# Layer 0's output product on two float16 parts for 28 of its 32 steps, with the weights' squares summed ahead

## The chip, the core and the metric

The kernel runs on one NeuronCore of a Trainium2 chip. The metric is the device time of one execution in microseconds; the median of three timed runs before the change is 1795.62 us (1794.34 to 1796.36). A core has a matrix engine (TensorE, PE in the profile; its weight loads are listed as PEld), a vector engine (VectorE, DVE), an activation engine (ScalarE, ACT), a general engine (GpSimd, POOL), a queue engine that mostly issues transfers (SyncE, SP), and 16 DMA engines shared by all queues. Each engine takes its instructions in the order of its own queue and waits on semaphores.

## The reference, cut to what matters

Two layers of a prefix model over 256 tokens and 256 context tokens, width 2048, branch width 4096. Layer 0 is a Fourier mixer, layer 1 an attention mixer. The change lies in the end of layer 0: the gate `silu(z)` and the output product `y @ w_out[0]`.

```
def _fourier_branch(h, w_in, w_mix):
    u, z = jnp.split(h @ w_in, 2, axis=-1)
    ...
    f = jnp.einsum('bngc,gcd->bngd', f, w_mix).reshape(b, n, D_BRANCH)
    return f * jax.nn.silu(z)

def reference(...):
    for i in range(DEPTH):
        shift, scale, gate = jnp.split((jax.nn.silu(c) @ ada_w[i] + ada_b[i])[:, None, :], 3, axis=-1)
        ...
        x = x + gate * (y @ w_out[i])
        if need_ctx:
            xc = xc + gate_c * (yc @ w_out[i])
    return _rmsnorm(x, final_g)
```

All is float32. The kernel keeps that accuracy on the matrix engine by writing each operand as a high part and a low part and summing three products (high x high, high x low, low x high).

## The kernel before, in words

**Products in parts.** `mm3` (lines 132 to 135) issues the three matmuls, 128x128 stationary by 128x512 moving (256 tokens of x beside 256 of the context). Two kinds of parts are in use. The float32r kind (`split`, `half_split`, lines 65 to 73): ACT casts to the high part (L66), DVE subtracts for the low part (L67); a half weight tile of 128x1024 takes two slots of the pool `wsp`, which has six. The float16 kind (`split16`, lines 122 to 127): ACT scales and casts (L125), DVE multiplies and subtracts (L126); both parts of a half tile share one slot. Float16 has few exponent bits, so it needs a power-of-two scale first: `squares` sums the squares of a weight tile on ACT (L81), `as_b` casts the sums to bfloat16 (L86), `all_sum` adds them over the partitions with small matmuls against ones (L93) into a PSUM tile of its own, and `weight_scale` makes the scale and its inverse with three tiny DVE operations (L117 to L119).

**The gate product (lines 802 to 874).** For each of 32 blocks of 128 branch columns, z = W_z^T h, on float16 parts. The first four blocks share weight tiles; then block b has its own 1 MB tile in the pool `raw` (three slots), loaded and squared two blocks ahead (`z_load`). A step is 16 k times three matmuls. At k = 6 of step b the scale of block b + 1 is made. `z_out` (L817 on) takes Silu of z on ACT (L820), multiplies the mixer's y by it on DVE (L821), and then draws a unit of the adaptive modulation. The results `ys` stay in the pool `yp`, 32 tiles of 128x512 float32.

**The modulation units (`ada_jobs`, lines 757 to 785).** 64 units, drawn by `next(ada)`. A unit loads 1 MB of the modulation weights (two tiles `zr` and `wa` in the gate stage, one `raw` tile later) and reduces it on DVE against rows of silu(c): four reductions of 128x1024 (L780), only two where the piece is the last (i = 3). The rows `cb` are loaded by POOL.

**The output product (lines 877 to 941).** 32 steps: two sweeps of 16, each over all 4096 rows of half of w_out's columns. Step i loads one `raw` tile of 1 MB, splits it to float32r parts (four `wsp` slots), and multiplies it with the parts of two tiles of y into eight PSUM tiles, all eight banks. `y_split0` makes these parts (L66 and L67 at 128x512) in slots of the pool `act` (33 slots, shared with the gate's h parts and temporaries), one step ahead, and again in the second sweep. In the last step of a sweep `evac0` adds each bank times the gate `gt0` to x on DVE and squares the result on ACT. From the twelfth step of a sweep on, POOL loads tiles of x. `ada_rate` says how many modulation units a step draws.

**Order.** Instructions get their places on an engine's queue by a list scheduler when the program is built; `tc.issue_after(ins)` forces what stands in the block behind `ins` on the same engine.

Of the kernel before, what the change touches and what calls it, by code (L numbers as in the profile page):

```python
# [17 lines left out]
P = 128  # L18
# [14 lines left out]
def tile_dit(ctx: ExitStack, tc: tile.TileContext, a: dict, out: bass.AP):  # L33
# [21 lines left out]
    def act(dt=F32):  # L55
        return actp.tile([P, 512], dt, tag="act", name="act")
# [8 lines left out]
    def split(h, l, src, eng=V):  # L65
        last_cast[0] = S.copy(h, src).ins  # L66
        last_sub[0] = eng.tensor_tensor(l, src, h.bitcast(F32), op=ALU.subtract).ins  # L67
# [47 lines left out]
    def weight_scale(b, ea):  # L115
        x, up, dn = tiny(I32), tiny(), tiny()
        V.tensor_scalar(x, all_sum(b).bitcast(I32), 24, 23, op0=ALU.logical_shift_right, op1=ALU.logical_shift_left)  # L117
        V.tensor_scalar(up.bitcast(I32), x, -1.0, 204.0 * 2**23, op0=ALU.mult, op1=ALU.add)  # L118
        V.tensor_scalar(dn.bitcast(I32), x, ea, 2.0**23, op0=ALU.add, op1=ALU.max)  # L119
        return up, dn  # L120

    def split16(t, i, up):
        w = wsp.tile([P, 2, 1024], F16, tag="ws", name="wf")
# [5 lines left out]
    def ws_split(t):  # L129
        return [half_split(t, i) for i in range(2)]  # L130
# [626 lines left out]
    def ada_jobs():  # L757
        for pieces in ((0,), (1, 2, 3)):
            for kh in range(2):
                cb = adap.tile([P, 2, 1024], F32, tag="cb", name="cb")  # L760
                with tc.issue_after(hs_end[2]):
                    nc.gpsimd.dma_start(cb, a["crow"][:, kh].broadcast_to([P, 2, 1024]))
                with tc.issue_after(hs_end[1]):
                    S.activation(cb, cb, AF.Silu)
                for i in pieces:
                    for fg in range(8):
                        for f in range(2):
                            q = slice(f * 1024, f * 1024 + 1024)
                            if f == 0 and not out0[0]:
                                wf = adat.tile([P, 1024], F32, tag="zr", name="zr", bufs=2)  # L770
                                nc.sync.dma_start(wf, a["adw"][i, kh, fg][:, q])
                            elif not out0[0]:
                                wf = wsp.tile([P, 1024], F32, tag="ws", name="wa")
                                nc.sync.dma_start(wf, a["adw"][i, kh, fg][:, q])
                            else:
                                if f == 0:
                                    w = raw(a["adw"][i, kh, fg])
                                wf = w[:, q]
                            for s in range(2 if i < 3 else 1):
                                V.tensor_tensor_reduce(junk if s == 0 and i < 3 else wf, wf, cb[:, s], 1.0, 0.0, ALU.mult, ALU.add, acc[:, i, kh, fg * 2 + f, s : s + 1])  # L780
                        if kh == 1 and fg == 7:
                            ada_done(i)
                        yield
        while True:
            yield
# [5 lines left out]
    adat = lay0.enter_context(tc.tile_pool(name="adat", bufs=1))  # L791
    junk = adat.tile([P, 1024], F32, name="junk")
    acc = adat.tile([P, 4, 2, KT, 2], F32, name="acc")
    with tc.tile_pool(name="yp", reuse_waits="tile", bufs=32) as ypool:
        ys = []
        for b in range(NB):
# [5 lines left out]
        def make_hs(k):  # L802
# [10 lines left out]
                hs_end[0] = V.scalar_tensor_tensor(l[:, q], t, sh0[:, k, s : s + 1], h[:, q], op0=ALU.add, op1=ALU.subtract).ins  # L813
            hs.append((h, l))

        if True:
            def z_out(b, o, dn):  # L817
                y = ys[b]
                z = act()
                S.activation(z, o, AF.Silu, scale=dn)  # L820
                V.tensor_tensor(y, y, z, op=ALU.mult)  # L821
                if b >= 4:
                    with tc.issue_after(hs_end[0]) if b < 8 else nullcontext():
                        for _ in range(0 if b in (12, 20) else 1):
                            next(ada)

            zt, sc, sb = {}, {}, {4 + i: as_b(nrm[:, 38 + 2 * i : 40 + 2 * i]) for i in range(2)}

            def z_load(b):
                if b < NB:  # L830
                    zt[b] = raw(a["wz"][b - 4])
                    if b > 5:
                        sb[b] = squares(zt[b], b)

            o4 = [psum() for _ in range(4)]
            for kg in range(4):
                wr = raw(a["wz0"][kg])
                w = []
                for i in range(2):
                    make_hs(kg * 4 + i * 2)  # L840
                    with tc.issue_after(hs_end[0]) if kg else nullcontext(), tc.issue_after(hs_end[1]) if kg else nullcontext():
                        w.append(split16(wr, i, up4))
                    make_hs(kg * 4 + i * 2 + 1)
                if kg == 3:
                    z_load(4)
                    sc[4] = weight_scale(sb[4], ea)
                for j in range(4):
                    k = kg * 4 + j
                    wh, wl = w[j // 2]
                    for b in range(4):  # L850
                        q = slice((j % 2) * 512 + b * P, (j % 2) * 512 + (b + 1) * P)
                        mm3(o4[b], wh[:, q], wl[:, q], hs[k][0], hs[k][1], k == 0, k == KT - 1)
            for b in range(4):
                with tc.issue_after(last_dma[0]):
                    nc.sync.dma_start(ys[b], fd[b])
            for b in range(4):
                z_out(b, o4[b], dn4)
            z_load(5)
            for b in range(4, NB):
                t, (up_, dn_) = zt.pop(b), sc.pop(b)  # L860
                w = [split16(t, i, up_) for i in range(2)]
                z_load(b + 2)
                with tc.issue_after(last_dma[0]):
                    nc.sync.dma_start(ys[b], fd[b])
                o = psum()
                for k in range(KT):
                    if k == 6 and b + 1 < NB:
                        with tc.issue_after(r):
                            sc[b + 1] = weight_scale(sb[b + 1], ea)
                    wh, wl = w[k // 8]  # L870
                    q = slice((k % 8) * P, (k % 8 + 1) * P)
                    r = mm3(o, wh[:, q], wl[:, q], hs[k][0], hs[k][1], k == 0, k == KT - 1)
                z_out(b, o, dn_)
            out0[0] = True


        x1, sqs = [], []
        yy = {}

        def y_split0(i):  # L880
            for j in range(2):
                h, l = act(F32R), act(F32R)
                split(h, l, ys[i % 16 * 2 + j])
                yy[i, j] = (h, l)

        def evac0(k, o):
            t = xin.pop(0)
# [18 lines left out]
        xin, sq_end, st_end, sums = [], [None], [None], []  # L906
        identr = act(F32R)[:, 0:P]
        S.copy(identr, ident)
        ada_rate = {2: 2, 4: 2, 6: 2, 8: 2, 10: 2, 14: 0, 15: 0, 16: 0, 18: 2, 20: 2, 22: 2, 25: 2, 26: 2, 27: 2, 28: 2, 29: 0, 30: 0, 31: 0}
        y_split0(0)  # L910
        for i in range(32):
            sw, kg = i // 16, i % 16
            if kg == 0:
                o = [psum() for _ in range(8)]
            w = ws_split(raw(a["wo0"][sw, kg]))
            if i < 31:
                y_split0(i + 1)
            else:
                wr = raw(a["wkv"][0])
                w0 = half_split(wr, 0)  # L920
            if kg >= 12:
                for k in range(sw * 8 + (kg - 12) * 2, sw * 8 + (kg - 12) * 2 + 2):
                    t = act()
                    nc.gpsimd.dma_start(t, a["xT"][:, k, :])
                    xin.append(t)
            with tc.issue_after(last_sub[0]) if i < 2 or 11 < i < 19 else nullcontext():
                for _ in range(ada_rate.get(i, 1)):
                    next(ada)
            edge = kg in (0, 15)
            for j, b in [(j, b) for b in range(8) for j in range(2)] if edge else [(j, b) for j in range(2) for b in range(8)]:  # L930
                q = slice(b * P, (b + 1) * P)
                last = i == 31 and (j, b) == (1, 7)
                if last:
                    sums.append(psum())
                    with tc.issue_after(e):
                        row_sums(0)
                        row_sums(1)
                with tc.issue_after(st_end[0]) if last else nullcontext():
                    e = mm3(o[b], w[j][0][:, q], w[j][1][:, q], *yy[i, j], kg + j == 0, kg * 2 + j == NB - 1)
                if kg == 15 and j == 1:  # L940
                    evac0(sw * 8 + b, o[b])
# [628 lines left out]
```

## Time and profile before

| | us |
|---|---|
| median of three timed runs | 1795.62 |
| the profiled execution, its own time | 1790.85 |
| its span (first to last instruction) | 1789.1 |
| gate product, from the Silu of the first blocks to that of the last | 372.15 to 661.10 |
| output product, first sweep | 662.55 to 838.50 |
| output product, second sweep | 838.50 to 1012.90 |

The profile is of one execution. A row for an instruction gives its start, its duration, the engine and the line, what it writes and reads, and in brackets how long the engine sat idle before it and what ended that. A row for a group gives the sum of its time, the mean of one in ns, and the idle time before. A matmul's duration includes the time in which the next already runs, so the distance from start to start is its price. A stretch gives the busy time of each engine between two times.

### The profile page before, as it was taken

Reading aid. Unit: us, or ns where it says so; the run is one execution under the profiler, and the core shown is the slowest. Engines: PE = TensorE matmul, PEld = TensorE weight load, DVE = VectorE, ACT = ScalarE, POOL = GpSimd, SP = SyncE. Lnnn points to the kernel's source line nnn. Section 1 sums busy time; section 2 is a strip of 40 time slices with the busy share of each in tenths; the row PEclk is TensorE's granted clock in tenths of the full one; section 3 lists DMA queues with packets and bytes.
Section 4 is the critical chain, followed back from the end, with each engine's and each line's share of the span. In section 5 each row is a group of like instructions: output and inputs, shape, how many; then the busy total and the mean of one; then the engine's idle time right before and its main releaser. Section 6 shows DMA issues by size and latency. Waiting matters only on the chain.

```text
span 1789.1 us, 25928 instructions
## 1 busy us (share of the span) xinstructions
PE 1752.3 (98%) x9514; PEld 1340.9 (75%) x9514; DVE 1399.3 (78%) x2406; ACT 977.5 (55%) x1701; POOL 213.5 (12%) x214
## 2 busy tenths in 40 slices
PE   6999999999999999999999999999999999999997
PEld 4679999544444448888888888788888878887886
DVE  5779888787776779776996563899999999997455
ACT  5545555464555453224222443687788778886343
POOL 0001111100000000000001000322213221234010
PEclk9999999999999999999999999999999999999999
DMA  9998998766666645863678322578888888887543
GB/s 394 417 353 256 274 278 237 300 229 216 232 211 238 227 143 212 321 243 118 227 267 321 119 94 99 173 198 213 219 200 207 212 212 206 213 213 269 192 168 142
DMA packets 210720, 405.16 MB, mean 226 GB/s; under 512 B 152672, under 2 KB 153072, under 8 KB 178848
## 3 DMA queue, kind: packets, MB, share of 16 engines
q1 hardware_dynamic: 186528, 365.49, 63.2%
q0 software_dynamic: 19920, 31.06, 6.8%
q10 hardware_dynamic: 4144, 6.95, 1.1%
q8 instruction: 75, 1.23, 0.3%
q14 instruction: 53, 0.43, 0.1%
HBM read 358.35 MB, written 12.59 MB: 207 GB/s over the span
## 4 chain that ended last, share of the span: by engine, by line
PE 57%; DVE 6%; DMA 4%; issue 2%; ACT 1%; SPq 0%; POOLq 0%; DVEq 0%; POOL 0%; ACTq 0%
PE ps L133 14%; PE ps L135 14%; PE ps L134 14%; PE ps L1234 5%; PE ps L1236 3%; DMA wa<-in_adw 2%; DMA ft<-f 1%; PE ps L1305 1%; PE ps L1270 1%; PE ps L1271 1%; PE ps L1306 1%; DVE junk L780 1%; DVE wl L67 1%; DVE f L1288 1%; DVE ps L1272 1%
## 5 line engine op out<-in xcount | busy, mean ns | idle before, releaser
L67 DVE TENSOR_TENSOR wl<-raw,wh 128x1024 fp32r<-128x1024 f32 x269 | 349.3, 1305 | 171.3 <-ACT wh L66 162.2
L66 ACT CAST wh<-raw 128x1024 fp32r<-128x1024 f32 x269 | 280.5, 1046 | 286.7 <-PE ps L134 198.8
L133 PE MATMUL ps<-act,wh 128*128 128x512 f32 x512 | 198.4, 390 | 1.5 <-ACT act L66 1.5
L134 PE MATMUL ps<-act,wh 128*128 128x512 f32 x512 | 199.2, 389 | 0.0
L134 PE MATMUL ps<-act,wf 128*128 128x512 f16 x512 | 194.0, 379 | 0.0
L135 PE MATMUL ps<-act,wf 128*128 128x512 f16 x512 | 191.0, 379 | 1.4 <-DVE wf L126 1.3
L133 PE MATMUL ps<-act,wf 128*128 128x512 f16 x512 | 189.8, 379 | 1.1 <-ACT act L812 0.3
L1234 PE MATMUL ps<-h,wh 128*128 128x512 f32 x512 | 184.8, 396 | 0.0
L135 PE MATMUL ps<-act,wl 128*128 128x512 f32 x512 | 184.2, 389 | 0.0
L1236 PE MATMUL ps<-h,wl 128*128 128x256 f32 x512 | 138.6, 281 | 0.0
L125 ACT ACTIVATE wf<-raw,tn 128x1024 f16<-128x1024 f32 x64 | 70.1, 1140 | 105.8 <-DVE tn L118 103.1
L134 PE MATMUL ps<-wl,h 128*128 128x512 f32 x320 | 126.7, 396 | 0.0
L135 PE MATMUL ps<-wh,h 128*128 128x512 f32 x320 | 125.3, 395 | 0.0
L133 PE MATMUL ps<-wh,h 128*128 128x512 f32 x320 | 124.0, 402 | 0.0
L133 PEld LDWEIGHTS ps<-act,wh 128*128 128x128 f32 x512 | 96.0, 188 | 22.1 <-ACT act L66 2.0
L1288 DVE SCALAR_TENSOR_TENSOR f<-p,sm,f 128x512 f16<-128x512 f32 x128 | 104.5, 836 | 9.5 <-ACT f L1287 9.2
L134 PEld LDWEIGHTS ps<-act,wh 128*128 128x128 f32 x512 | 96.1, 188 | 20.1
L135 PEld LDWEIGHTS ps<-act,wl 128*128 128x128 f32 x512 | 96.1, 188 | 19.9
L1234 PEld LDWEIGHTS ps<-h,wh 128*128 128x128 f32 x512 | 96.2, 188 | 18.9
L1275 ACT ACTIVATE p<-ps,mx 128x512 f32<-128x512 f32 x128 | 87.9, 689 | 38.3 <-DVE mx L1272 32.2
L1287 ACT ACTIVATE f<-p,sm 128x512 f16<-128x512 f32 x128 | 87.8, 717 | 31.6 <-DMA ft<-f 13.6
L126 DVE SCALAR_TENSOR_TENSOR wf<-raw,tn,wf 128x1024 f16<-128x1024 f32 x64 | 79.6, 1280 | 30.7 <-ACT wf L125 30.7
(372 smaller groups left out, 4160.7 us busy)
## 6 DMA issues: line engine op xcount, KB each, us to landing
raw<-in_wz SPq DMA_DIRECT2D x64, 1024.0 KB, 5.1
raw<-in_adw SPq DMA_DIRECT2D x38, 1024.0 KB, 6.1
raw<-in_awp SPq DMA_DIRECT2D x32, 1024.0 KB, 12.8
raw<-in_wo SPq DMA_DIRECT2D x32, 1024.0 KB, 5.1
raw<-in_wq SPq DMA_DIRECT2D x32, 1024.0 KB, 5.0
raw<-in_wu SPq DMA_DIRECT2D x32, 1016.0 KB, 6.6
raw<-in_wo1b SPq DMA_DIRECT2D x16, 1024.0 KB, 4.9
zr<-in_adw SPq DMA_DIRECT2D x26, 512.0 KB, 4.0
```

The lines of the kernel that those rows point to most:

```text
L66: last_cast[0] = S.copy(h, src).ins
L67: last_sub[0] = eng.tensor_tensor(l, src, h.bitcast(F32), op=ALU.subtract).ins
L125: last_cast[0] = S.activation(w[:, 0], src, AF.Copy, scale=up).ins
L126: last_sub[0] = V.scalar_tensor_tensor(w[:, 1], src, up, w[:, 0], op0=ALU.mult, op1=ALU.subtract).ins
L133: PE.matmul(o, wh, xh, start=start, stop=False)
L134: PE.matmul(o, wh, xl, start=False, stop=False)
L135: return PE.matmul(o, wl, xh, start=False, stop=stop).ins
L1234: PE.matmul(o[0], wh[:, q], hx1[k], start=k == 0, stop=k == KT - 1)
L1236: PE.matmul(o[0][:, 0:N], wl[:, q], hx1[k][:, 0:N], start=False, stop=False)
L1275: S.activation(pt[tb], so[tb], AF.Exp, bias=mx[:, tb : tb + 1], scale=-1.0, accum_out=sm[:, tb : tb + 1])
L1287: S.activation(f[:, 0:512], pt[tb], AF.Copy, scale=sm[:, tb : tb + 1])
L1288: V.scalar_tensor_tensor(f[:, 512:1024], pt[tb], sm[:, tb : tb + 1], f[:, 0:512], op0=ALU.mult, op1=ALU.subtract)
```

## The change

Steps 0 to 13 of each sweep (28 of 32) use float16 parts for the weights and for y; steps 14 and 15 keep float32r. One scale serves all weights of a sweep and one serves all y, so that the products of a sweep can be summed in the same banks. y's parts in steps 14 and 15 are multiplied by both scales, and `gt0` takes the inverse.

To know the scales in time, the weights of w_out are loaded a first time by POOL in half tiles (two pieces of 128x512 each, into `act` slots) and squared with a sum on ACT: 36 half tiles beside the gate product (one after even blocks, two after odd, blocks 4 to 27), 28 in steps 0 to 13 of the first sweep. The squares of y 0 to 27 are summed behind `z_out`. The first sweep's sums are made in gate steps 29 and 30, the second sweep's in step 14.

The float16 parts of y are kept for the second sweep, in place of y itself. The parts of steps 0 and 1 are made in gate step 31. The scale of gate block b + 1 is made at k = 1 in place of k = 6. The last 24 modulation units are put in another order, so that a unit with two reductions comes between those with four, and `ada_rate` is given anew (38 units in the 32 steps, as before).

```
+    def sum_scale(b):
+        s, x, up = tiny(), tiny(I32), tiny()
+        V.tensor_scalar(s, all_sum(b), 2.0**-70, None, op0=ALU.max)
+        V.tensor_scalar(x, s.bitcast(I32), 24, 23, op0=ALU.logical_shift_right, op1=ALU.logical_shift_left)
+        V.tensor_scalar(up.bitcast(I32), x, -1.0, 204.0 * 2**23, op0=ALU.mult, op1=ALU.add)
+        return x, up
...
+                order = [(i, fg) for i in pieces for fg in range(8)]
+                if kh == 1 and len(pieces) == 3:
+                    thirds = [(3, fg) for fg in range(8)]
+                    order = order[:4] + [o for pair in zip(order[4:12], thirds) for o in pair] + order[12:16]
...
+    def scan_sums():
+        while pend:
+            t, j = pend.pop(0)
+            S.activation(t, t, AF.Square, accum_out=scn[:, j : j + 1])
+
+    def scan_loads(n):
+        for j in [next(scans) for _ in range(n)]:
+            for q in range(2):
+                t = act()
+                c = (j % 2 * 2 + q) * 512
+                nc.gpsimd.dma_start(t, a["wo0"][j // 32, j % 32 // 2][:, c : c + 512])
+                pend.append((t, j * 2 + q - 64 * (j >= 36)))
...
+    def half_scale(sw, sums_):
+        x, up = sum_scale(sums_[0])
+        if sw == 0:
+            xy, uy = sum_scale(sums_[1])
+            keep(ysc[:, 0:1].bitcast(I32), xy)
+            keep(ysc[:, 1:2], uy)
+        up_ = keep(ysc[:, 2 + 3 * sw : 3 + 3 * sw], up)
+        both, dn = ysc[:, 3 + 3 * sw : 4 + 3 * sw], ysc[:, 4 + 3 * sw : 5 + 3 * sw]
+        V.tensor_tensor(both, up_, ysc[:, 1:2], op=ALU.mult)
+        V.tensor_scalar(dn.bitcast(I32), x, ysc[:, 0:1].bitcast(I32), -27.0 * 2**23, op0=ALU.add, op1=ALU.add)
+        return up_, both, dn
...
+        def y_split0(i):
+            for j in range(2):
+                k = i % 16 * 2 + j
+                if k < 28:
+                    if i < 16:
+                        t = (ypool if k else actp).tile([P, 1024], F16, tag="y" if k else "act", name="y")
+                        h, l, up = t[:, 0:512], t[:, 512:1024], ysc[:, 1:2]
+                    else:
+                        yy[i, j] = yy[i - 16, j]
+                        continue
+                else:
+                    h, l, up = act(F32R), act(F32R), osc[i // 16][1]
+                last_cast[0] = S.activation(h, ys[k], AF.Copy, scale=up).ins
+                last_sub[0] = V.scalar_tensor_tensor(l, ys[k], up, h if k < 28 else h.bitcast(F32), op0=ALU.mult, op1=ALU.subtract).ins
+                yy[i, j] = (h, l)
...
                 V.tensor_tensor(y, y, z, op=ALU.mult)
+                if b < 28:
+                    ysq[b] = z
+                for i in [i for i in ysq if i < b]:
+                    S.activation(ysq.pop(i), ys[i], AF.Square, accum_out=scn[:, 72 + i : 73 + i])
...
-                    if k == 6 and b + 1 < NB:
+                    if k == 1 and b + 1 < NB:
                         with tc.issue_after(r):
                             sc[b + 1] = weight_scale(sb[b + 1], ea)
+                    if (k, b) == (4, 29):
+                        with tc.issue_after(r):
+                            hsum = half_sum(0)
+                    if (k, b) == (12, 30):
+                        with tc.issue_after(r):
+                            osc.append(half_scale(0, hsum))
+                    if (k, b) == (10, 31):
+                        with tc.issue_after(r):
+                            y_split0(0)
+                            y_split0(1)
...
                 z_out(b, o, dn_)
+                scan_sums()
+                scan_loads(1 + b % 2 if b < 28 else 0)
...
-        ada_rate = {2: 2, 4: 2, 6: 2, 8: 2, 10: 2, 14: 0, 15: 0, 16: 0, 18: 2, 20: 2, 22: 2, 25: 2, 26: 2, 27: 2, 28: 2, 29: 0, 30: 0, 31: 0}
-        y_split0(0)
+        ada_rate = {**{i: 2 for i in (*range(6, 10), *range(17, 25))}, **{i: 0 for i in (14, 15, 16, 29, 30, 31)}}
...
-            w = ws_split(raw(a["wo0"][sw, kg]))
-            if i < 31:
+            wr = raw(a["wo0"][sw, kg])
+            w = [split16(wr, j, osc[sw][0]) for j in range(2)] if kg < 14 else ws_split(wr)
+            if sw == 0:
+                scan_sums()
+                scan_loads({0: 3, 3: 3, 6: 1, 7: 1, 8: 1, 9: 1, 10: 3, 12: 3}.get(i, 2) if i < 14 else 0)
+            if i == 14:
+                osc.append(half_scale(1, half_sum(1)))
+            if kg == 14:
+                q = gt0[:, sw * 8 : sw * 8 + 8].rearrange("p k s -> p (k s)")
+                V.tensor_scalar(q, q, osc[sw][2], None, op0=ALU.mult)
+            if i in range(1, 31):
                 y_split0(i + 1)
```

`half_sum` reduces the columns of the sums on DVE and casts them for `all_sum`; `keep` is a copy of one column; a rate not given is 1.

## What was predicted

> **What bounds the kernel now.** I read the page first (busy times, chain), then the stretches of the two stages that the change touches, then single instructions there.
>
> ```profile
> span 1789.1 us, 25928 instructions
> PE 1752.3 (98%) x9514; PEld 1340.9 (75%) x9514; DVE 1399.3 (78%) x2406; ACT 977.5 (55%) x1701; POOL 213.5 (12%) x214
> ...
> PE 57%; DVE 6%; DMA 4%; issue 2%; ACT 1%; SPq 0%; POOLq 0%; DVEq 0%; POOL 0%; ACTq 0%
> ```
>
> PE works 98% of the span and carries most of the chain: time comes from shorter matmuls or from the few gaps between them. The stretches (us, then PE, PEld, DVE, ACT, POOL busy, granted clock, DMA share, GB/s):
>
> ```profile
> 372.15:661.10 288.95, 287.47 (x1373) 129.70 (x1371) 217.04 (x371) 142.77 (x220) 1.06 (x2) 1.00 0.64 222
> 523.28:533.69 10.41, 10.41 (x51) 4.74 (x50) 8.04 (x14) 5.14 (x9) 0.00 (x0) 1.00 0.53 190
> 564.92:661.10 96.18, 94.70 (x448) 41.88 (x446) 71.45 (x120) 41.85 (x64) 0.00 (x0) 1.00 0.61 213
> 662.55:838.50 175.95, 175.95 (x775) 145.47 (x776) 135.71 (x207) 56.68 (x73) 4.81 (x9) 1.00 0.61 221
> 838.50:1012.90 174.40, 174.40 (x779) 144.58 (x779) 136.51 (x214) 53.18 (x71) 5.89 (x11) 1.00 0.62 227
> ```
>
> The gate product runs in steps of 48 matmuls (one step is the second row, PE full). The output product follows, in two sweeps of 16 steps (last two rows), PE full, ACT a third busy. So inside the output product only the matmul's own pitch can be won; at the joint and in the late gate steps there are gaps.
>
> **The pitch.** Gate product (float16 parts), first and last of 38 consecutive matmuls; output product (float32r parts), two casts that each wait for PE to free a half step's weight slot, three half steps of 24 matmuls apart:
>
> ```profile
> 547.84 0.38 PE L133 MATMUL ps<-act,wf 128*128 128x512 f16 x1
> ...
> 555.82 0.38 PE L134 MATMUL ps<-act,wf 128*128 128x512 f16 x1
> ```
>
> ```profile
> 804.29 1.06 ACT L66 CAST wh<-raw 128x1024 fp32r<-128x1024 f32 x1 [4.38 <-PE ps L134]
> ...
> 820.61 1.05 ACT L66 CAST wh<-raw 128x1024 fp32r<-128x1024 f32 x1 [4.38 <-PE ps L134]
> ```
>
> Float16: 7.98 us / 37 = 215.7 ns. Float32r: 16.32 us / 72 = 226.7 ns. The difference is 11.0 ns, and the weight loads beside them differ too:
>
> ```profile
> L134 PEld LDWEIGHTS ps<-act,wh 128*128 128x128 f32 x512 | 96.1, 188 | 20.1
> L134 PEld LDWEIGHTS <-wf 128*128 128x128 f16 x512 | 50.0, 98 | 56.2
> ```
>
> 28 steps x 48 x 11.0 ns = 14.8 us less. This is the main term; both shapes are exactly those of the change (128x128 stationary, 128x512 moving), the clock is 1.00 in both, so I take it whole. Its low bound is nothing.
>
> [...]
>
> **The joint.** The last gate matmul and the first of the output product:
>
> ```profile
> 660.68 0.38 PE L135 MATMUL ps<-act,wf 128*128 128x512 f16 x1
> ...
> 662.55 0.74 PE L133 MATMUL ps<-act,wh 128*128 128x512 f32 x2 [1.49 <-ACT act L66]
> ```
>
> PE waits 1.49 us for the first y split, which is queued after the last Silu on ACT. The change issues the splits of steps 0 and 1 (y 0 to 3, long finished) during gate step 31, behind its 11th k. So this gap goes: -1.5 us. What is late next is weight tile 0, whose scale is asked for in step 30, ten us before.
>
> **The late gate steps.** The third row above holds 9 steps that would take 9 x 10.41 = 93.7 us; it is 2.5 us longer. What such a step shows:
>
> ```profile
> 575.90 0.39 PE L135 MATMUL ps<-act,wf 128*128 128x512 f16 x1 [0.18 <-DVE wf L126]
> ...
> 587.05 0.39 PE L135 MATMUL ps<-act,wf 128*128 128x512 f16 x1 [0.57 <-DVE wf L126]
> ```
>
> ```profile
> 578.84 1.22 DVE L780 CUSTOM_DVE_ANT_0 junk<-wa,cb 128x1024 f32<-128x1024 f32 x1 [1.80 <-DMA wa<-in_adw]
> ```
>
> ```profile
> 584.53 2.19 ACT L125 ACTIVATE wf<-raw,tn 128x1024 f16<-128x1024 f32 x2 [6.09 <-DVE tn L118]
> ```
>
> DVE waits for a modulation tile, does its four reductions, and only then the three tiny operations of the next weight's scale; ACT, idle for 6.09 us, splits the weight just too late. The scale moves from k = 6 to k = 1, 15 matmuls (3.2 us) earlier, ahead of that burst. Its two small matmuls sit in PE's own queue, but the sum of squares they read belongs to a weight squared one step before, so PE should not wait. Between 0 and 2.5 us are won; I take 2.0, nearer the upper end because the DVE idle time of 1.80 us is itself room for the three operations.
>
> **What is added to ACT, DVE, POOL and the DMA engines.** Rows for the prices (busy us, mean ns):
>
> ```profile
> L125 ACT ACTIVATE wf<-raw,tn 128x1024 f16<-128x1024 f32 x64 | 70.1, 1140 | 105.8 <-DVE tn L118 103.1 <-DVE tn L119 2.7
> L126 DVE SCALAR_TENSOR_TENSOR wf<-raw,tn,wf 128x1024 f16<-128x1024 f32 x64 | 79.6, 1280 | 30.7 <-ACT wf L125 30.7
> L896 ACT ACTIVATE act<-act 128x512 f32<-128x512 f32 x14 | 8.8, 631 | 10.4 <-DVE act L891 10.4
> L81 ACT ACTIVATION_READ_ACCUMULATOR sq<-raw 128x1 f32 x49 | 9.3, 190 | 0.0
> L119 DVE TENSOR_SCALAR tn<-tn,ea 128x1 int32<-128x1 int32 x26 | 5.3, 203 | 0.0
> L780 DVE CUSTOM_DVE_ANT_0 raw<-raw,cb 128x1024 f32<-128x1024 f32 x76 | 91.5, 1219 | 7.1 <-DMA raw<-in_adw 6.8
> L67 DVE TENSOR_TENSOR act<-y,act 128x512 fp32r<-128x512 f32 x64 | 42.3, 684 | 3.1 <-ACT act L66 1.5 <-PE ps L134 1.2 <-PE ps L135 0.4
> L1288 DVE SCALAR_TENSOR_TENSOR f<-p,sm,f 128x512 f16<-128x512 f32 x128 | 104.5, 836 | 9.5 <-ACT f L1287 9.2
> ```
>
> A Square of 128x512 with its sum is not shown; it costs between 0.63 us (L896) and 0.63 + 0.19 = 0.82 (accumulator read not hidden). In the gate steps ACT has 5.14 busy of 10.41 us. A step gains one y Square and two or four scan Squares: 3 to 5 of them, 1.9 to 4.1 us, so 7.0 to 9.2 of 10.41. It fits, and as the scale no longer holds ACT back, the weight splits stay ahead.
>
> In the output product's first sweep DVE has per step 2 x 1.28 (weights), two y parts at 0.68 to 0.84, and at most four reductions at 1.22 to 1.30: 8.8 to 9.4 of 48 x 0.2157 = 10.35 us. In steps 17 to 24 the y parts are gone (reused), and two modulation tiles of 4 and 2 reductions come: 2.56 + 6 x 1.22 to 1.30 = 9.9 to 10.4. That is at the edge for eight steps. But a float16 weight takes one of the six wsp slots per half instead of two, so the splits can run two steps ahead; a debt of 8 x 0.1 us is nothing to that. The other debt is the raw slots. Loads now:
>
> ```profile
> act<-in_xT POOLq DMA_DIRECT2D x32, 256.0 KB, 7.5
> y<-fd SPq DMA_DIRECT2D x32, 256.0 KB, 5.2
> raw<-in_wo SPq DMA_DIRECT2D x32, 1024.0 KB, 5.1
> ```
>
> ```profile
> 700.00:800.00 100.00, 100.00 (x442) 82.59 (x441) 76.66 (x113) 28.56 (x32) 4.81 (x9) 1.00 0.77 282
> ```
>
> 282 GB/s at a share of 0.77 puts the ceiling near 366. The 36 half tiles beside the gate product are 18.9 MB over 24 steps (250 us): 75 on 222 GB/s, share 0.64 to 0.86. In the output product three raw tiles a step (17 to 24) are 3.1 MB / 10.35 us = 304 GB/s; with a scan half tile (steps 6 to 9) 355. Close to the ceiling for four steps, with two steps of lead to spend. I charge 1.5 us for all of this, bounds 0 and 9 (0.75 us in each of 12 such steps).
>
> The turn between the sweeps: evacuation keeps DVE full, and the second scale (step 14) needs a ninth PSUM tile, so it waits for the first evacuated bank.
>
> ```profile
> 835.91 0.87 DVE L891 SCALAR_TENSOR_TENSOR act<-ps,gt,act 128x256 f32<-128x256 f32 x2
> 836.70 0.68 DVE L898 TENSOR_TENSOR act<-act 128x512 f32<-128x512 f32 x1
> 837.29 0.87 DVE L891 SCALAR_TENSOR_TENSOR act<-ps,gt,act 128x256 f32<-128x256 f32 x2
> 838.09 1.21 DVE L67 TENSOR_TENSOR wl<-raw,wh 128x1024 fp32r<-128x1024 f32 x1
> ```
>
> One bank costs DVE 1.38 us, so the first bank is out some 2.5 us into step 15 and the scale, about ten operations of 0.2 us (L119), 2 us later, with 6 us of the step left. The weight's low part already comes last here (838.09) without a gap on PE, because the high-part matmuls go first. Cost 0 to 3 us, inside the charge above.
>
> **Sum.** -14.8 - 1.5 - 2.0 + 1.5 = -16.8 us. The profiled execution took 1790.85 us (span 1789.1 plus 1.75 around it), so 1774.0; the timed median, 1795.62, lies 4.8 higher, and the same difference gives 1778.8, rounded to 1779.
>
> **Rivals.**
>
> 1. Given back in the output product (chance 0.14): DVE and the raw slots cannot keep step in 6 to 9 and 17 to 24 and the turn stalls. For it: 304 to 355 GB/s, DVE at 96 to 100% in eight steps. Against: the lead of two steps, and ada rate 0 in steps 14 to 16. Back come 9 us less the 1.5 charged: 1786.
>
> 2. Slower (0.13): the scans bar ACT in the gate stage. ACT takes its queue in order; behind a Square whose half tile has not landed stand the next weight's casts, behind these DVE's low parts, behind these PE. For it: loads from POOL took 7.5 us where SP's of the same size took 5.2, up to four are issued together, and DMA share rises to 0.86. Against: each has a whole step (10.4 us) from issue to use, and the casts, which now end just when PE needs them, move up by 3.2 us. It decides from a loss of 0.85 us in each of 24 steps (20.4 us); at 1.0 us the time is 1779 + 24 = 1803.
>
> [...]
>
> 3. The pitch does not follow the type in this stage (0.07): 226.7 ns stays, only joint and gate gaps are won: 1795.6 - 3.5 + 1.5 = 1793.6. Against it: the two rows have the same shape and clock.
>
> **How the numbers follow.** The forecast has 0.66, its own range 1775 to 1783 (gate gain 0 to 2.5, charge 0 to 4, spread of the median 1). The range 1774 to 1793 takes in rival 1 and most of rival 3. A measurement here tells about 0.2%, 3.6 us, from no change. Faster: 0.66 + 0.14 + 0.02 of rival 3 = 0.82; same 0.06 (rival 3, and a mild rival 2); slower 0.12.
>
> **What would show it.** Right: float16 matmuls in steps 0 to 13 and 16 to 29 at 215.7 ns, steps of 10.35 us; no gap at the joint; gate steps of 10.41 to the end; the weight casts (L125's line) starting within 2 us of a gate step's start. Wrong: ACT waiting for DMA on act before a Square, gate steps above 10.5 us, PE waiting for the low parts in steps 6 to 9, 16, or 17 to 24.

## The result and the profile after

The kernel got slower. The changed kernel takes 1811.68 us (median of 4 runs, 1806.36 to 1812.01) where the kernel before takes 1795.72 (4 runs, 1794.34 to 1796.36): ratio 1.0083, 95% interval 1.0064 to 1.0102. The forecast was 1779. The profiled execution took 1811.7 us with a span of 1809.9, 20.8 more than before.

The head of the page after; PE's busy time is what it was (1752.3 before), so neither the shorter matmuls nor the longer span show in it:

```profile
span 1809.9 us, 26397 instructions
PE 1752.0 (97%) x9517; PEld 1222.7 (68%) x9517; DVE 1391.8 (77%) x2401; ACT 1061.6 (59%) x1989; POOL 279.7 (15%) x342
```

The two stages as stretches, first before, then after: from the Silu of gate step 4 to that of step 31, and from there to the first sum over x1 behind the output product (length, then PE, PEld, DVE, ACT, POOL busy, granted clock, DMA share, GB/s).

```profile
377.54:661.10 283.56, 282.08 (x1348) 127.25 (x1346) 211.65 (x363) 138.10 (x210) 1.06 (x2) 1.00 0.64 221
661.10:1010.40 349.30, 347.85 (x1534) 287.69 (x1535) 272.73 (x418) 110.51 (x144) 10.71 (x20) 1.00 0.61 225
```

```profile
378.99:688.29 309.30, 294.27 (x1369) 129.31 (x1368) 218.52 (x385) 198.55 (x411) 50.95 (x96) 0.98 0.80 276
688.29:1027.80 339.51, 331.56 (x1516) 165.05 (x1515) 255.14 (x389) 133.00 (x227) 25.72 (x48) 0.99 0.69 257
```

| us | before | after | difference |
|---|---|---|---|
| up to the Silu of step 4 | 377.5 | 379.0 | +1.5 |
| gate stage | 283.6 | 309.3 | +25.7 |
| output product | 349.3 | 339.5 | -9.8 |
| the rest | 778.7 | 782.1 | +3.4 |

In the gate stage PE sits idle for 309.30 - 294.27 = 15.0 us (before 1.5), the stage holds some 18 matmuls of the output product that now come ahead of the last Silu (3.9 us, missing from the second row), and the clock is at 0.98 of full (added up over stretches of 4 us, 5.1 us are lost to it). With 13.5 us more of idle time that is some 22 of the 25.7 us. In the output product the float16 gain is there, but 8.0 us of PE idle time (before 1.5) and 0.99 of clock stand against it. DMA works at 0.80 of the gate stage instead of 0.64, and the two modulation loads land later, zr after 4.9 us in place of 4.0, wa after 6.3 in place of 4.9 (transfers issued in the gate stage: KB each, median us to landing; before, then after):

```profile
wa<-in_adw SPq DMA_DIRECT2D x24, 512.0 KB, 4.9
```

```profile
wa<-in_adw SPq DMA_DIRECT2D x24, 512.0 KB, 6.3
```

**Where the gate step comes from.** Single instructions of one gate step after (start, duration, engine; in brackets the idle time before and what ended it):

```profile
499.33 0.33 SPq L787 DMA_DIRECT2D zr<-in_adw  x1
499.70 0.42 SPq L790 DMA_DIRECT2D wa<-in_adw  x1
506.39 1.22 DVE L796 CUSTOM_DVE_ANT_0 junk<-wa,cb 128x1024 f32<-128x1024 f32 x1 [2.11 <-DMA wa<-in_adw]
510.07 1.22 DVE L796 CUSTOM_DVE_ANT_0 zr<-zr,cb 128x1024 f32<-128x1024 f32 x1
511.22 0.15 DVE L117 TENSOR_SCALAR tn<-ps 128x1 int32<-128x1 int32 x1
511.33 0.33 SPq L787 DMA_DIRECT2D zr<-in_adw  x1
511.71 0.52 SPq L790 DMA_DIRECT2D wa<-in_adw  x1
512.63 2.17 ACT L137 ACTIVATE wf<-raw,tn 128x1024 f16<-128x1024 f32 x2
515.14 0.39 PE L147 MATMUL ps<-act,wf 128*128 128x512 f16 x1 [0.71 <-DVE wf L138]
```

This is a ring that does not pass through PE. SP issues a zr tile once the last reduction of a unit has freed a zr slot, and the wa tile of the next unit stands behind it in SP's queue. DVE waits for wa, does four reductions in order, and frees zr again: 499.33 to 511.33, a period of 12.00 us where PE needs 10.41. In it lie 0.37 us from zr to wa, 6.7 us until DVE can start on wa, and 4.9 us of DVE. The next weight's scale (L117) stands behind the four reductions, so the ring also times the casts and in the end PE. The kernel before has the same ring:

```profile
584.26 0.33 SPq L771 DMA_DIRECT2D zr<-in_adw  x1
584.68 0.38 SPq L774 DMA_DIRECT2D wa<-in_adw  x1
589.31 1.22 DVE L780 CUSTOM_DVE_ANT_0 junk<-wa,cb 128x1024 f32<-128x1024 f32 x1 [1.13 <-DMA wa<-in_adw]
594.73 0.33 SPq L771 DMA_DIRECT2D zr<-in_adw  x1
```

0.42 + 4.63 + 5.42 = 10.47 us: it was closed already, at 0.06 us over PE's step. This is one of its short periods; the four others between 568 and 622 us are 10.6 to 11.2 us long.

**The clock behind a gap.** A PE wait after, and the stretches that follow it:

```profile
479.74 0.39 PE L145 MATMUL ps<-act,wf 128*128 128x512 f16 x1 [3.15 <-ACT wf L137]
```

```profile
480.00:484.00 4.00, 3.26 (x11) 1.02 (x10) 3.53 (x5) 4.00 (x10) 1.08 (x2) 0.68 0.78 247
484.00:488.00 4.00, 4.00 (x18) 1.77 (x17) 3.97 (x8) 0.69 (x2) 0.00 (x0) 0.89 0.95 317
488.00:492.00 4.00, 4.00 (x21) 1.77 (x19) 2.36 (x5) 3.75 (x8) 0.04 (x1) 1.00 0.85 298
```

3.26 x 0.32 + 4 x 0.11 = 1.5 us of clock are lost behind 3.9 us of waiting (3.15 and 0.72); from 481.5 to 484.9 us the matmuls start 0.43 us apart in place of 0.22. The same happens behind two more waits of the gate stage (the clock is 0.91 over 420 to 440 and over 600 to 620) and behind the longest of the output product (5.06 us; 0.83 over 760 to 780). The length of the waits alone does not decide it in this execution: the dip of 600 to 620 follows waits of 2.00 and 0.71 us, the one of 420 to 440 waits of 1.20 and 0.72 us, while waits of 1.32 and 0.71 us at 747.87 leave the clock at 1.00.

```profile
605.71 0.39 PE L145 MATMUL ps<-act,wf 128*128 128x512 f16 x1 [2.00 <-ACT wf L137]
```

```profile
608.00:612.00 4.00, 4.00 (x12) 1.43 (x11) 3.97 (x9) 3.27 (x8) 0.97 (x2) 0.61 0.67 229
```

### The profile page after: what moved, and what is told of

It reads as the page before. It is cut to its first block, busy times and chain, and to the rows that moved or that the text cites. A ratio compares the mean times of both kernels' runs of the same rounds, so it can differ in the third digit from the quotient of the medians.

```text
span 1809.9 us, 26397 instructions
## 1 busy us (share of the span) xinstructions
PE 1752.0 (97%) x9517; PEld 1222.7 (68%) x9517; DVE 1391.8 (77%) x2401; ACT 1061.6 (59%) x1989; POOL 279.7 (15%) x342
## 5 line engine op out<-in xcount | busy, mean ns | idle before, releaser
L67 DVE TENSOR_TENSOR wl<-raw,wh 128x1024 fp32r<-128x1024 f32 x213 | 280.9, 1324 | 153.3 <-ACT wh L66 128.7
L66 ACT CAST wh<-raw 128x1024 fp32r<-128x1024 f32 x213 | 222.5, 1046 | 191.9 <-PE ps L146 158.0
L145 PE MATMUL ps<-act,wf 128*128 128x512 f16 x512 | 191.9, 383 | 8.5 <-ACT wf L137 6.9
L147 PE MATMUL ps<-act,wf 128*128 128x512 f16 x512 | 192.9, 383 | 7.4 <-DVE wf L138 7.4
L146 PE MATMUL ps<-act,wf 128*128 128x512 f16 x512 | 196.0, 383 | 0.0
L145 PEld LDWEIGHTS <-wf 128*128 128x128 f16 x960 | 94.3, 98 | 133.9 <-ACT wf L137 23.1
L147 PEld LDWEIGHTS <-wf 128*128 128x128 f16 x960 | 94.2, 98 | 128.5 <-DVE wf L138 14.8
L145 PE MATMUL ps<-y,wf 128*128 128x512 f16 x448 | 170.5, 382 | 7.4 <-ACT wf L137 7.2
L146 PE MATMUL ps<-y,wf 128*128 128x512 f16 x448 | 170.8, 381 | 0.5 <-DVE y L883 0.4
L146 PEld LDWEIGHTS <-wf 128*128 128x128 f16 x960 | 94.4, 98 | 109.3 <-issue 3.0
L147 PE MATMUL ps<-y,wf 128*128 128x512 f16 x448 | 165.7, 379 | 0.7 <-DVE wf L138 0.7
L137 ACT ACTIVATE wf<-raw,nrm 128x1024 f16<-128x1024 f32 x56 | 61.2, 1139 | 135.7 <-DMA raw<-in_wo 108.8
L824 POOL DMA_DIRECT2D act<-in_wo x128 | 68.6, 537 | 258.6 <-ACT act L817 81.6
```

What stands on the lines that cost most here:

```text
L137: last_cast[0] = S.activation(w[:, 0], src, AF.Copy, scale=up).ins
L145: PE.matmul(o, wh, xh, start=start, stop=False)
L146: PE.matmul(o, wh, xl, start=False, stop=False)
L147: return PE.matmul(o, wl, xh, start=False, stop=stop).ins
L824: nc.gpsimd.dma_start(t, a["wo0"][j // 32, j % 32 // 2][:, c : c + 512])
```

## The experiments

Three theories of the gate stage. **ACT** (rival 2 of the prediction): the scans' Squares hold up the casts. **Hand-over**: the y Square, which waits for DVE's product, holds them up. **Ring**: the scans' transfers and the earlier scale lengthen the ring above. Each time is one run beside one run of the kernel before on the same chip, unless said otherwise; idle is PE's, worked out from the two stretches as above.

| run | us (before) | gate, its idle | output, its idle |
|---|---|---|---|
| before | 1795.7 | 283.6, 1.5 | 349.3, 1.5 |
| after | 1811.7 | 309.3, 15.0 | 339.5, 8.0 |
| e1 | 1814.3 (1791.2) | 304.8, 17.4 | 346.9, 11.4 |
| e2 | 1807.7 (1791.2) | 307.3, 15.7 | 338.7, 7.1 |
| e3 | 1794.0 (1791.2) | 301.1, 12.1 | 330.6, 1.1 |
| e4 | 1827.4 (1791.2) | 313.3, 23.7 | 349.7, 1.6 |
| e5 | 1787.8 (1792.3) | 299.8, 11.1 | 330.4, 0.9 |
| e6 | 1779.4 (1792.3) | 284.5, 1.1 | 333.0, 1.1 |
| e7 | 1789.8 (1792.3) | 297.1, 8.9 | 330.2, 0.9 |
| e8 | 1810.4 (1792.3) | 309.6, 16.7 | 340.2, 7.5 |
| e9 | 1799.9 (1796.4) | 293.3, 9.1 | 349.2, 1.4 |
| e10 | 1821.1 (1796.4) | 311.1, 19.6 | 348.5, 10.0 |
| e11 | 1789.0 (1796.4) | 283.2, 1.7 | 345.4, 9.4 |
| e12 | 1789.9 (1796.4) | 282.2, 0.9 | 349.2, 1.5 |
| e13 | 1786.2 (1796.1) | 282.3, 0.7 | 345.7, 10.3 |
| e14 | 1785.0 (1796.1) | 281.2, 0.0 | 345.9, 9.7 |
| e15 | 1778.5 (1796.1) | 282.1, 0.7 | 334.8, 1.5 |
| e16 | 1778.0 (1794.1) | 281.3, 0.0 | 334.5, 1.2 |
| e17 | 1776.4 (1794.1) | 281.7, 0.5 | 334.7, 1.4 |
| e18 | 1780.2 (1793.7) | 292.9, 6.4 | 330.6, 0.9 |

### Taking the scans apart: e1 to e4

e1 leaves out the 72 scan transfers beside the gate product; their Squares read a resident tile, and the first sweep's scale comes from a constant:

```
+                if j >= 36:
+                    nc.gpsimd.dma_start(t, a["wo0"][j // 32, j % 32 // 2][:, c : c + 512])
+                pend.append((t, t if j >= 36 else r_bc, j * 2 + q - 64 if j >= 36 else 100))
```

> The 72 scan transfers beside the gate product are left out; their Squares stay on ACT, on a tile that is already there (the sums are constants of the right size). Theory 'ring' (the gate step is a ring: SP issues zr and behind it wa, wa lands, DVE does four reductions, the zr slot comes free, SP issues the next zr; the scan transfers lengthen wa's landing from 4.9 to 6.3 us): landing back near 5 us, 27 gate steps 281 to 288 us in place of 309, whole time 1785 to 1793. Rival 'ACT' (the Squares in ACT's queue delay the weight casts): gate steps stay at 300 to 309, whole time 1803 to 1812.

e2 keeps the transfers and leaves out their Squares (`if j >= 36: pend.append(...)`).

> The transfers beside the gate product stay, their 72 Squares on ACT are left out (sums are constants of the right size). 'Ring': wa still lands after 6 us or more, gate steps 300 to 309, whole time 1800 to 1812. 'ACT': gate steps back to 281 to 288, whole time 1785 to 1793.

e3 leaves out all 64 scan half tiles, transfers and Squares, in both stages; the Squares of y stay.

> All 64 scan half tiles left out, transfers and Squares, in the gate stage and in the first sweep (sums are constants of the right size); the y Squares stay. Both theories: gate steps near 284 us. It shows what the float16 pitch is worth with nothing paid for it: 28 steps x 0.53 us = 14.8 us, and the stall of 7 us near steps 6 to 8 of the output product gone if the scan transfers caused it. Ring and no other loss: whole time 1773 to 1778. If the stall stays: 1780 to 1785.

e4 is the kernel before with the 72 transfers added, into tiles that nobody reads:

```
+                for q in range(2 * (1 + b % 2) if b < 28 else 0):
+                    nc.gpsimd.dma_start(act(), a["wo0"][b // 16, b % 16][:, q * 512 : q * 512 + 512])
```

> The kernel before, with the 72 transfers beside the gate product added and nothing else (nobody reads them). 'Ring': gate steps from 283.6 to 297 to 309 us, time 1803 to 1816. 'ACT': no change, 1790 to 1797.

Neither half of the scans in the changed kernel brings the gate stage back: 304.8 without the transfers, 307.3 without the Squares, and still 301.1 without either. So in these kernels something besides the scans costs most of it. Yet in the kernel before the transfers alone cost 29.7 us. One of e4's long steps:

```profile
505.66 0.33 SPq L771 DMA_DIRECT2D zr<-in_adw  x1
506.08 0.38 SPq L774 DMA_DIRECT2D wa<-in_adw  x1
514.93 1.23 DVE L780 CUSTOM_DVE_ANT_0 junk<-wa,cb 128x1024 f32<-128x1024 f32 x1 [5.34 <-DMA wa<-in_adw]
520.35 0.33 SPq L771 DMA_DIRECT2D zr<-in_adw  x1
521.82 0.39 PE L133 MATMUL ps<-act,wf 128*128 128x512 f16 x1 [3.22 <-ACT wf L125]
```

wa takes 8.85 us to its use, the period is 14.69 us, and PE waits 3.22. ACT does nothing new in e4, so the ACT theory is not needed for this loss. The ring theory as first put had e1 at 1785 to 1793 and missed by 21 us: it knew only the transfers. POOL's transfers delay SP's here: wa's median to landing is 5.5 us in e4, where they alone are new, against 4.9 before, and 6.3 in the kernel after.

### The other cost: e5 to e7 and e9

e5 is e3 without the Squares of y too (its scale from a constant).

> No scans as in e3_no_scans, and the 28 y Squares left out as well (their sums are constants of the right size). Theory 'hand-over' (in ACT's queue a y Square stands ahead of the next weight's casts and waits for DVE's multiplication of that y, which stands behind the four reductions on DVE; that puts about 1.3 us more into every gate step): gate 27 steps from 301 to 284 to 289 us, time 1774 to 1780. Rival 'scale at k = 1' or the reordered units cost it: gate stays 298 or more, time 1789 or more.

e7 is e3 with these Squares two steps later (`if i < b - 2`).

> No scans as in e3_no_scans; the y Squares stay but each is done three steps after its y in place of one, so that it never waits for DVE. 'Hand-over': as without y Squares, gate 284 to 290, time 1775 to 1782. If ACT's mere time for them (0.8 us a step) were the cause: gate stays near 300, time 1790 to 1796.

e6 is e3 with the scale back at k = 6:

```
-                    if k == 1 and b + 1 < NB:
+                    if k == 6 and b + 1 < NB:
```

> No scans as in e3_no_scans, and the scale of the next gate block back at k = 6. 'Hand-over': nothing changes, since DVE does the scale behind the reductions in both: gate 297 to 304, time 1789 to 1797. 'Scale at k = 1': gate 284 to 289, time 1776 to 1781.

e9 is the reverse edit alone, in the kernel before: k = 1.

> The kernel before, with nothing but the next block's scale asked for at k = 1 in place of k = 6. Theory 'order' (asking for it earlier gives another order on DVE, in which the first reduction, which waits for wa, stands ahead of a weight's low part; e6_no_scans_k6 won 16 us by undoing it): gate from 283.6 to 292 to 302 us, time 1799 to 1811. If the loss needs the y Squares too: gate 283 to 286, time 1789 to 1796.

The hand-over theory fell: with no y Square at all the gate stage is 299.8. The move of the scale is the second cost: 301.1 to 284.5 when it is undone, 283.6 to 293.3 when it is done alone. How it lengthens the ring is seen in e3 (k = 1), then e6 (k = 6):

```profile
474.12 1.23 DVE L796 CUSTOM_DVE_ANT_0 junk<-wa,cb 128x1024 f32<-128x1024 f32 x1 [2.46 <-DMA wa<-in_adw]
475.27 1.28 DVE L138 SCALAR_TENSOR_TENSOR wf<-raw,tn,wf 128x1024 f16<-128x1024 f32 x1
480.03 0.15 DVE L117 TENSOR_SCALAR tn<-ps 128x1 int32<-128x1 int32 x1
480.14 0.33 SPq L787 DMA_DIRECT2D zr<-in_adw  x1
480.51 0.42 SPq L790 DMA_DIRECT2D wa<-in_adw  x1
485.81 1.23 DVE L796 CUSTOM_DVE_ANT_0 junk<-wa,cb 128x1024 f32<-128x1024 f32 x1 [1.92 <-DMA wa<-in_adw]
```

```profile
476.97 0.33 SPq L787 DMA_DIRECT2D zr<-in_adw  x1
478.42 2.48 DVE L138 SCALAR_TENSOR_TENSOR wf<-raw,tn,wf 128x1024 f16<-128x1024 f32 x2 [1.10 <-ACT wf L137]
482.17 1.22 DVE L796 CUSTOM_DVE_ANT_0 junk<-wa,cb 128x1024 f32<-128x1024 f32 x1 [1.27 <-DMA wa<-in_adw]
487.59 0.33 SPq L787 DMA_DIRECT2D zr<-in_adw  x1
```

In e6 the weight's two low parts run back to back while wa is on its way. In e3 the order on DVE puts a reduction that waits for wa ahead of the second low part, so that part's 1.2 us lie inside the ring. From the start on wa to the next zr it takes 6.02 us (in e6 5.42, with the product of y and the gate in it, which e3 does behind), and wa comes later too; the period is 0.37 + 5.30 + 6.02 = 11.69 us against e6's 10.62. And the scale, asked for at k = 1, still comes after all four reductions (480.03): the move did not bring it ahead of the burst. Over the gate stage this order, a low part between the two reductions of wa, stands 10 times in e3, 10 in e1 and 13 in e9, but once in the kernel after and never in e6 and the kernel before.

### Opening the ring: e8, e10 to e12

e8 is the changed kernel with three zr slots (`bufs=3`; the scrap output of the reductions moves to older space to make room).

> The changed kernel whole, with three zr slots in place of two (the reductions' unused product goes to an idle tile as bfloat16, which frees the space). 'Ring' (SP's zr issue waits for its slot, wa stands behind it): DVE no longer waits for wa, gate from 309 to 288 to 296, time 1788 to 1797. 'Hand-over' alone: gate 303 to 309, time 1803 to 1812.

e10 is the changed kernel, whole, with k = 6.

> The changed kernel whole, with the scale back at k = 6. If the move and the scan transfers cost by themselves and add up: gate from 309 to 290 to 300 us (the scan transfers still lengthen wa's landing), time 1786 to 1800. If the scans alone already hold the ring: gate 303 to 309, time 1800 to 1810. If the move was all: gate 284 to 288, time 1776 to 1784.

e11 is e10 with wa issued ahead of the next zr on SP; e12 puts the same into the kernel before:

```
+                                with tc.issue_after(wa_end[0]) if wa_end[0] else nullcontext():
+                                    nc.sync.dma_start(wf, a["adw"][i, kh, fg][:, q])
...
+                                wa_end[0] = nc.sync.dma_start(wf, a["adw"][i, kh, fg][:, q]).ins
```

> As e10_k6, and SP issues each wa ahead of the next zr (an ordering edge; the work is the same). 'Ring': wa no longer stands behind the zr that waits for the end of the four reductions, it is issued some 2.5 us earlier; DVE's wait for wa falls from some 40 us to under 15, gate 283 to 290, time 1776 to 1788. If wa's landing time isn't what holds the step: no change against e10_k6.

> The kernel before with the same ordering edge alone. 'Ring': the late gate steps of 10.6 to 11.1 us go to 10.4, gate from 283.6 to 281, time 2 to 3 us under that of the kernel before. Otherwise: no change, within 1 us.

A third zr slot changes nothing (309.6): wa still stands behind a zr that waits. In its trace zr is issued 0.04 us after the last reduction, at 497.54, and wa 0.38 us behind it, as with two slots. With k = 6 alone the scans hold the ring as in e4 (311.1). So in the changed kernel undoing the move wins nothing (gate stage 309.3 to 311.1, time 1811.7 to 1821.1), and the two costs do not add up: the transfers hold its ring by themselves, and e1 and e3, built anew without them, get the other order on DVE and with it the other cost. With wa first the gate stage is 283.2 with all scans in it. e11's ring:

```profile
500.81 0.33 SPq L791 DMA_DIRECT2D wa<-in_adw  x1
501.19 0.42 SPq L788 DMA_DIRECT2D zr<-in_adw  x1
507.78 1.22 DVE L797 CUSTOM_DVE_ANT_0 junk<-wa,cb 128x1024 f32<-128x1024 f32 x1
511.21 0.33 SPq L791 DMA_DIRECT2D wa<-in_adw  x1
```

wa is asked for during the reductions and, 6.97 us later, DVE takes it without waiting; the period is 10.40, PE's own. DMA is as busy as ever (0.83 of the stage), and the transfers land no sooner (wa's median is 7.0 us, in the kernel after 6.3); they are asked for sooner. In the kernel before (e12) the edit is worth 1.3 us of gate stage; its one time is 6.5 us below its neighbour, but that kernel itself ranged from 1791.6 to 1796.8 in seven runs on one chip, so the time doesn't tell.

### The first sweep: e13 to e17

e11 still lacked 10 us: its output product takes 345.4 us, e6's 333.0, with one PE wait of 7.42 us. e13 evens out the loads of the first sweep (its lines are below), e14 goes further (no step with two units there; two in 17 to 28, the pairs of a whole and a half unit first; two scan half tiles in each of steps 0 to 13), e15 is e11 without any scans:

```
+        ada_rate = {**{i: 2 for i in (5, 10, *range(17, 27))}, **{i: 0 for i in (14, 15, 16, 29, 30, 31)}}
...
+                scan_loads({2: 3, 5: 1, 10: 1, 12: 3}.get(i, 2) if i < 14 else 0)
```

> As e11 (scale at k = 6, wa issued ahead of the next zr), with the first sweep's loads evened out: two modulation units in steps 5 and 10 only (e11: steps 6 to 9), ten steps of two in the second sweep (17 to 26), scans one in steps 5 and 10, three in 2 and 12, two elsewhere. Theory (raw slots): in e11's steps 6 to 9 three 1 MB tiles a step share three raw slots, so the next weight is not loaded ahead and PE waits 7.4 us at 740.49. Then that wait goes: output product 345.4 to 336-340 us, time 1789 to 1780-1784. Rival (the DMA ceiling: all loads of the first sweep together are too many): PE still waits above 4 us there, output product 342 or more, time 1786 or more. Gate stage 283 to 285 in both.

> As e13, but no step of the first sweep draws two modulation units; two in all of steps 17 to 28, the pairs of a whole and a half unit first; scans two in each of steps 0 to 13. Raw slots theory: no PE wait of over 1 us in the first sweep; the second sweep loses at its end where two whole units stand in a step (steps 25 to 28, 12.6 us of DVE in 10.35), 0 to 4 us: output product 334 to 340, time 1778 to 1784. Rival (DMA ceiling or ACT's queue): as e13's rival, 1786 or more.

> Leaves out all 64 scan half tiles (the scale comes from a constant of the right size); scale at k = 6 and wa issued ahead of the next zr. The floor of the change: gate stage 282 to 284 (e6 284.5, before 283.6), output product 331 to 333 as in e6, time 1776 to 1779. If the gate stage does not fall below 284, the edge is worth nothing without the scans; if it falls to 281, the ring already cost the kernel before 2 us.

Moving loads did not help: PE's waits in the first sweep and at the turn fall from 9.4 us (e11) to 7.9 (e13) and 3.9 (e14), but the units that went to the second sweep bring 2.4 and 5.7 us there, and the stage stays at 345.7 and 345.9. Without scans it is 334.8, so they are the cause in some way. e13's longest wait shows which. Issue of the weight's tile, the last y split ahead of it, its cast, PE:

```profile
710.59 0.33 SPq L50 DMA_DIRECT2D raw<-in_wo  x1
...
724.32 0.72 ACT L883 ACTIVATE y<-y,nrm 128x512 f16<-128x512 f32 x1 [0.82 <-DVE y L884]
724.94 2.17 ACT L137 ACTIVATE wf<-raw,nrm 128x1024 f16<-128x1024 f32 x2
726.13 0.61 PE L145 MATMUL ps<-y,wf 128*128 128x512 f16 x1 [5.88 <-ACT wf L137]
```

The cast starts 14.35 us after its tile was asked for (the longest landing of a raw tile at that place is 9.3 us), and ACT waited for nothing ahead of it but hand-overs from DVE: since 709 it had worked off y splits and scan Squares of steps to come. e16 is e11 with these placed behind the casts of their own step, e17 the same with e13's rates; each is timed in 4 runs against 7 of the kernel before:

```
+            wc = last_cast[0], last_sub[0]
             if sw == 0:
-                scan_sums()
+                with tc.issue_after(wc[0]):
+                    scan_sums()
...
-                y_split0(i + 1)
+                with tc.issue_after(wc[0]), tc.issue_after(wc[1]):
+                    y_split0(i + 1)
```

> As e11 (scale at k = 6, wa ahead of the next zr, the change's own rates), and in the output product the scan Squares and the y splits of a step are placed behind that step's weight casts on ACT and DVE. Theory (run-ahead): in e11 and e13 ACT worked off scans and y splits of several steps to come before the next weight's casts, and the scans' transfers ran at about 400 GB/s until 720 us and delayed the weights; paced, ACT reaches the casts in time: the 7.4 us wait at 740 goes, output product 345.4 to 335-339 us, time 1779 to 1783. Rival (raw slots): the wait in steps 6 to 9 stays above 4 us, output product 341 or more, time 1785 or more. Either way faster than before by 0.4% or more.

> As e16 with e13's even rates (two units in steps 5, 10 and 17 to 26). Run-ahead theory: no PE wait of over 1.5 us in the first sweep, 2.4 us of waits in the second as in e13: output product 336 to 339, time 1778 to 1783, equal to e16 within 3 us. Raw slots theory: 3 to 6 us faster than e16.

e16: 1778.01 us (1774.8 to 1780.82), ratio to before 0.9912, interval 0.9895 to 0.9929. e17: 1776.37 us (1772.54 to 1778.93), ratio 0.9896, 0.9878 to 0.9915. Both beat both kernels; they compute everything that the changed kernel computes. e16's stretches:

```profile
375.85:657.14 281.29, 281.25 (x1351) 128.01 (x1350) 216.48 (x382) 199.06 (x411) 48.87 (x91) 1.00 0.83 299
657.14:991.60 334.46, 333.26 (x1535) 166.68 (x1533) 259.42 (x395) 133.99 (x227) 27.96 (x52) 1.00 0.72 267
```

ACT, DVE and DMA carry as much as in the kernel after; PE is full in both stages and the clock at 1.00. It was the order, not the amount. The edit orders ACT and DVE at once, and DMA moves its bytes more evenly with it (GB/s in the 16th to 20th of the page's 40 slices: 364, 284, 297, 143, 266 in e11; 350, 330, 253, 221, 293 in e16), perhaps because a later Square frees its tile later; which of these counts most was not tried apart. The rates make no difference beyond the scatter.

### The move once more: e18

e18 is e16 with the scale at k = 1.

> As e16 (wa ahead of the next zr, paced first sweep, the change's own rates) but with the scale at k = 1 as the change has it. If the move k = 6 to k = 1 costs only because the ring had no slack, the gate stage stays at 281 to 284 us and the time at 1776 to 1781. If it costs by itself (e6 to e3: 16.6 us, e9: 9.7 us in the gate stage), the gate stage is 287 us or more and the time 1783 or more.

```profile
377.46:670.37 292.91, 286.48 (x1362) 128.64 (x1361) 217.75 (x386) 196.45 (x410) 50.32 (x94) 0.99 0.81 289
```

PE is idle for 6.4 us in the gate stage (e16: 0.0), and the stage holds 11 matmuls of the output product, so it is 9 us longer for its own work; both stages together are 623.5 us against 615.8. A low part stands between the two reductions of wa 15 times (e16: 5). By the stage, the move costs by itself. By the time, 1780.24, it would be the other theory, because the rest took 777.4 us in this execution (e16 781.4) at the same work. One run doesn't settle the size.

## Why the prediction was wrong, point by point

- **Pitch (-14.8): right.** With PE not held up, e16's output product has 347.85 - 333.26 = 14.6 us less of PE busy time at the same count of matmuls. Rival 3 is out.
- **Joint (-1.5): right in kind.** The wait of 1.49 us is gone in e16; in the kernel after two of 0.16 and 0.43 us remain.
- **Late gate steps (-2.0 by moving the scale): this step failed, in sign.** It took the order from the place in the program ("ahead of that burst"): the scale still runs behind three or four of the four reductions, and in e3 and e9 a low part is drawn in among them. It costs 9.7 us of gate stage in the kernel before (e9) and 14 us over both stages without scans (e3 against e6). In the changed kernel this cost is covered by the next one (e10). The 2.5 us at stake were those of the ring, and opening it wins up to that: 281.2 to 283.2 us of gate stage in e11, e13, e14, e16 and e17, 283.6 before.
- **Additions (charge 1.5, bounds 0 to 9): this step failed, in place and size, and it alone is enough for the loss in the gate stage (e10).** The gate stage was priced by each engine's busy share ("It fits") and by the sum of GB/s. The time from wa's issue to its use was in neither, though the row that was quoted for something else, DVE waiting 1.80 us for wa, was this ring at its limit. Transfers cost 22 us of PE idle time there (e4), in a kernel whose ring already lay 0.06 us and more above the step.
- **Rival 2 (slower, 1803)** had the sign and, through later landings and the DMA share, half of the cause, but the wrong carrier: Squares on ACT that wait for their half tile. In the gate stage of the kernel after ACT waits 0.7 us in all for such tiles, DVE 41.2 us for wa. The casts wait for the scale, the scale for DVE, DVE for wa. e5 left the y Squares out and e7 moved them; they won 1.3 and 4.0 us of 17.5.
- **Rival 1 (steps 6 to 9)** came true beside it: 6.5 us more PE idle time in the output product, but from the order of work on ACT and DVE. DVE's share and the raw slots, which it named, were not the reason: e16 has the same rates and none of it.
- **The clock** was not in the sum. Each of the three dips in the gate stage cost some 1.5 to 1.8 us more.
- The sum itself, -16.8 us, is what e16 reaches, with the scale left at k = 6 and two orders that the change does not have: -17.1 in the two stages, 1778.0 us.

Not settled: why the rest, with the same work, varies from 777.4 to 783.6 us between these kernels, and so what made 3.4 us of the loss after; and what share ACT's order has in the gate stage. e1 has the scans' Squares there and hardly any of their transfers, e3 neither, and e1's PE is idle for 5.3 us more. It waits 10.7 us for ACT's casts (e3: 3.0): at 519.7 us, for instance, the scale is ready, but two Squares of a later weight, queued behind a scan's, run first, and the casts start at 521.68. In the kernel after, leaving the Squares out wins nothing of that (e2: 15.7 us idle against 15.0).

## What to carry to other kernels

Before adding transfers to a stage, follow one load around: from its issue, behind what it stands in the issuing queue, to landing, to its use, to the slot that it frees. Here that ring took as long as the step (10.47 us against 10.41), and no share of idle time on any engine was room (e4: 29.7 us more gate stage with DMA at 0.72 of it); another slot didn't help while the load stood behind one that waits (e8: 309.6 us against 309.3), asking for it earlier did (e11: 283.2). Work that isn't needed soon should be tied behind the work that is (output product 345.4 us in e11, 334.5 in e16): the order found at build time had run it ahead (e13), and an earlier place in the program was not an earlier place in the queue (e3's scale at 480.03).

## What the runs showed of the hardware

- In the kernel after, some 8 matmuls started 0.43 us apart in place of 0.22 behind PE waits of 3.15 and 0.72 us (479.74 above), of 2.00 and 0.71 (605.71) and of 1.20 and 0.72 (421.79), and none did behind waits of 1.32 and 0.71 us (747.87). The first of these dips cost about 1.5 us.
- In e16 DMA ran at a share of 1.01 for 20 us with PE busy for all of them (the stretch behind the joint, columns as above):

```profile
660.00:680.00 20.00, 20.00 (x94) 9.06 (x93) 13.28 (x21) 11.78 (x22) 5.93 (x11) 1.00 1.01 396
```
